# The norms' constant matrix and nineteen other tiles get other places in SBUF

## The chip, the cores and the metric

The kernel runs on one core of a Trainium2 chip. The time is device microseconds of one execution; three executions of the kernel before took 1021.14 to 1021.57 us, with a median of 1021.51 us.

## The reference

Two decoder layers over 256 tokens of width 1024, in float32. Each layer is: half a SwiGLU FFN, a token mixer beside four heads of cross-attention on a memory of 256 tokens, half a SwiGLU FFN. The mixer of the first layer is an mLSTM, that of the second a sliding-window attention.

```python
mem_kv = rms_norm(mem, mem_norm_g) @ mem_w_kv
for i in range(DEPTH):
    x = x + 0.5 * swiglu(rms_norm(x, ffn1_norm_g[i]), ffn1_w_in[i], ffn1_w_out[i])
    hn = rms_norm(x, mix_norm_g[i])
    ...
    x = x + jnp.concatenate([y_tok, y_mem], axis=-1) @ w_out
    x = x + 0.5 * swiglu(rms_norm(x, ffn2_norm_g[i]), ffn2_w_in[i], ffn2_w_out[i])
```

rms_norm(x, g) is x * rsqrt(mean(x*x) + 1e-6) * g, swiglu(x) is (silu(gate) * up) @ w_out with gate and up from x @ w_in (1024 x 5632), and w_out is 2816 x 1024.

## The kernel before

**Matrix products.** Activations lie with features on partitions, 256 tokens in the free dimension. Each float32 factor is split into two float32r parts: weights come from DRAM into a tile wr, ScalarE casts it to wh, VectorE subtracts to get wl; the normed activations are xh and xl, and other activations are split into tiles of the pool up, all named u. A product is three matmuls: wl by xh, wh by xh, wh by xl, each of 128 rows, 128 loaded columns and 256 streamed columns. In `nc.tensor.matmul(out, a, b)` a is loaded into the array (LDWEIGHTS in the profile) and b streams. The profile names a matmul out<-b,a: the streamed operand first, the loaded one after the comma. Most groups load the weights (out<-xh,wl) and stream the activations. Groups with rows=True, in the memory projection and the mixers, load the activations and stream the weights (out<-wl,xh).

**Norms.** The scale of a norm is a sum over features, so over partitions. Norm.square and Norm.fold add up the squares of a token's features per partition (tile acc, a pool of one buffer) and split the result into a tile of the pool up; Norm.chain then multiplies by a 128x128 matrix whose every element is 1/1024, the tile onesr: `nc.tensor.matmul(z, onesr, self.sums[:, i], ...)` for two halves i. There are seven norms, so 14 matmuls that load onesr. The groups that use the norm's result have already begun when these two matmuls run, since the scale is applied to the product; so on TensorE the two stand in the middle of a stream of weight products.

**Small float32 work.** Transposes stream the identity, which is the first 128 columns of the tile con; the cross-attention streams its keys kT and loads its values vM; the sliding-window heads load identb and stream maskb to put a mask into PSUM. These, with onesr, are the tiles of the pool cst that TensorE reads.

**The order.** The program is first noted operation by operation (class Rehearsal). plan() simulates the engines and puts out an order; perform() emits the operations in this order. A tile is a Slot until then: its real tile is asked of its pool when the first operation that names it is emitted (Slot.real). In a pool with several buffers a tag's tiles follow each other through them. In a pool with one buffer, each tag has one place, and the pool gives out places in the order in which it is asked. These pools are cst (20 tags: constants and other tiles that are there once), ap1 (acc) and gp (acol).

**SBUF.** cst begins at byte 16512 of each partition and ends at 29120. Below, a phase is a place modulo 512 bytes, which is the length of one loaded block of 128 float32 columns; the blocks of a tile lie at multiples of 512 from its start, so all of them have one phase. wh and wl lie at phase 0; xh, xl and every u lie at phase 448; these pools do not move.

Of the kernel before, what the change touches and what calls it, by code (L numbers as in the profile page):

```python
# [191 lines left out]
class Rehearsal:  # L192
# [33 lines left out]
    def perform(self, order):  # L226
        nc = self.tc.nc

        def real(x):
            return x.real() if isinstance(x, View) else x  # L230

        for n in order:
            op = self.ops[n]
            getattr(getattr(nc, op.engine), op.kind)(*map(real, op.args), **{k: real(x) for k, x in op.kw.items()})  # L234
# [1261 lines left out]
```

## Time and profile before

| what | before |
|---|---|
| median of three executions | 1021.51 us |
| profiled execution, its own time | 1021.53 us |
| its span, first to last instruction | 1019.7 us |
| mean granted TensorE clock | 0.999 |
| PE busy | 1013.6 us (99%), 8560 matmuls |
| PEld (weight loads) busy | 997.1 us (98%) |
| DVE busy | 664.6 us (65%) |
| ACT busy | 532.0 us (52%) |
| POOL busy | 26.9 us (3%) |

The span is divided like this, by the matmuls in it: memory projection to 32 us, first FFN to about 225, the mLSTM mixer to about 357, second FFN to about 546, third to about 720, the sliding-window mixer to about 838, fourth FFN to the end. The view of stretches gives, for a stretch from A to B us, its length, each engine's busy time in it, in brackets the number of its instructions that touch it, then the granted clock, the share of the DMA engines and GB/s. The duration that the profile gives to a matmul (some 280 ns) is modelled from start to end through a pipeline, and the next one starts long before; what a stream of them costs is the distance from start to start.

### The profile page before, as it was taken

To read this page: it belongs to the slowest core of one execution; us is meant where nothing else is said; L and a number is where in the kernel's file an instruction comes from. 1 tells how busy PE (TensorE), PEld (TensorE's weight loads), DVE (VectorE), ACT (ScalarE), POOL (GpSimd) and SP (SyncE) were. 2 spreads that over 40 slices of the span, in tenths; PEclk is the share of its full clock that TensorE was granted. 3 is DMA by queue.
4 is the path that set the end of the run, shared out by engine and by line. 5 is a ranking of instruction groups with operands and counts; after the bars stand their busy time and mean duration, and the time that the engine had idled before them with its cause. 6 is when DMAs were issued, how large, how long until landed. Compare 5 with 4: busy or idle time off the path is not lost.

```text
span 1019.7 us, 20571 instructions
## 1 busy us (share of the span) xinstructions
PE 1013.6 (99%) x8560; PEld 997.1 (98%) x8560; DVE 664.6 (65%) x1080; ACT 532.0 (52%) x779; POOL 26.9 (3%) x27
## 2 busy tenths in 40 slices
PE   9999999999999999999999999999999999999998
PEld 7999999999999999999999999999998899999998
DVE  6976656678756776655657756556677777656551
ACT  7754544546646644444445444445478765444430
POOL 0020000000000000000000000000113000000000
PEclk9999999999999999999999999999999999999999
DMA  9966665766454476655666666566533437665540
GB/s 322 291 191 200 193 194 173 198 191 180 140 170 145 144 230 186 186 178 175 188 202 189 187 186 187 166 194 192 172 104 125 142 113 223 186 187 176 185 156 22
DMA packets 173204, 182.70 MB, mean 179 GB/s; under 512 B 7124, under 2 KB 168328, under 8 KB 173112
## 3 DMA queue, kind: packets, MB, share of 16 engines
q1 hardware_dynamic: 171872, 179.60, 57.5%
q8 instruction: 67, 1.10, 0.4%
q10 hardware_dynamic: 1016, 1.58, 0.4%
q0 software_dynamic: 224, 0.22, 0.1%
q14 instruction: 25, 0.20, 0.1%
HBM read 180.32 MB, written 1.05 MB: 178 GB/s over the span
## 4 chain that ended last, share of the span: by engine, by line
PE 98%; DMA 1%; SPq 0%; DVE 0%; ACT 0%; issue 0%
PE bank L234 98%; DMA wr<-in_mem_w_kv_dram 1%; SPq L234 0%; DVE wl L234 0%; ACT wh L234 0%; DVE t L234 0%
## 5 line engine op out<-in xcount | busy, mean ns | idle before, releaser
L234 DVE TENSOR_TENSOR wl<-wr,wh 128x1024 fp32r<-128x1024 f32 (+1 forms) x349 | 414.7, 1191 | 282.7 <-ACT wh L234 281.2
L234 ACT CAST wh<-wr 128x1024 fp32r<-128x1024 f32 (+1 forms) x349 | 356.7, 1024 | 413.8 <-PE bank L234 394.7
L234 PE MATMUL bank<-xh,wh 128*128 128x256 f32 x1544 | 432.5, 280 | 0.0
L234 PE MATMUL bank<-xh,wl 128*128 128x256 f32 x1544 | 432.2, 280 | 0.0
L234 PE MATMUL bank<-xl,wh 128*128 128x256 f32 x1544 | 432.0, 280 | 0.0
L234 PE MATMUL bank<-u,wh 128*128 128x256 f32 x1792 | 314.3, 280 | 0.0
L234 PEld LDWEIGHTS bank<-xh,wl 128*128 128x128 f32 x1544 | 293.0, 190 | 0.0
L234 PEld LDWEIGHTS bank<-xl,wh 128*128 128x128 f32 x1544 | 291.6, 189 | 0.1
L234 PEld LDWEIGHTS bank<-xh,wh 128*128 128x128 f32 x1544 | 289.9, 188 | 0.1
L234 PEld LDWEIGHTS bank<-u,wh 128*128 128x128 f32 x1792 | 272.7, 188 | 1.4 <-issue 1.4
L234 PE MATMUL bank<-u,wl 128*128 128x256 f32 x896 | 250.7, 280 | 0.0
L234 PEld LDWEIGHTS bank<-u,wl 128*128 128x128 f32 x896 | 169.8, 190 | 0.5 <-issue 0.5
L234 PE MATMUL bank<-wh,xh 128*128 128x256 f32 x208 | 58.8, 283 | 0.0
L234 PE MATMUL bank<-wh,xl 128*128 128x256 f32 x208 | 58.8, 283 | 0.0
L234 PE MATMUL bank<-wl,xh 128*128 128x256 f32 x208 | 58.5, 281 | 0.0
L234 DVE TENSOR_TENSOR t<-bank,rb 128x256 f32<-128x256 f32 x88 | 36.6, 420 | 14.2 <-PE bank L234 13.9
L234 DVE TENSOR_TENSOR u<-t,u 128x512 fp32r<-128x512 f32 (+1 forms) x59 | 40.4, 685 | 0.3
L234 PEld LDWEIGHTS bank<-wh,xh 128*128 128x128 f32 x208 | 39.1, 188 | 0.1
L234 PEld LDWEIGHTS bank<-wl,xh 128*128 128x128 f32 x208 | 39.0, 188 | 0.1
L234 PEld LDWEIGHTS bank<-wh,xl 128*128 128x128 f32 x208 | 39.0, 188 | 0.1
L234 DVE TENSOR_TENSOR t<-t,bank 128x256 f32<-128x256 f32 x88 | 32.9, 414 | 1.1 <-ACT t L234 1.1
L234 POOL TENSOR_TENSOR col<-col,mhalf 128x4 f32<-128x4 f32 (+2 forms) x15 | 21.8, 1452 | 296.2 <-DVE col L234 296.2
(134 smaller groups left out, 582.0 us busy)
## 6 DMA issues: line engine op xcount, KB each, us to landing
wr<-in_ffn_w_in_dram SPq DMA_DIRECT2D x176, 512.0 KB, 4.5
wr<-in_ffn_w_out_dram SPq DMA_DIRECT2D x80, 512.0 KB, 3.7
wr<-in_a_w_in_dram SPq DMA_DIRECT2D x28, 512.0 KB, 3.7
wr<-in_b_w_in_dram SPq DMA_DIRECT2D x14, 512.0 KB, 4.5
wr<-in_a_w_out_dram SPq DMA_DIRECT2D x12, 512.0 KB, 3.3
wr<-in_b_w_out_dram SPq DMA_DIRECT2D x12, 512.0 KB, 3.4
wr<-in_ffn_w_out_dram SPq DMA_DIRECT2D x16, 256.0 KB, 2.7
wr<-in_mem_w_kv_dram SPq DMA_DIRECT2D x7, 512.0 KB, 7.2
```

What stands on the lines that cost most here:

```text
L234: getattr(getattr(nc, op.engine), op.kind)(*map(real, op.args), **{k: real(x) for k, x in op.kw.items()})
```

## The change

Before the first operation is emitted, every slot that is the first of its tag in a pool with one buffer asks for its real tile, in the order in which the tags were first named in the text. Before, they asked in the order of the plan.

```diff
@@ perform
+        for slots in self.slots.values():
+            if slots[0].pool.bufs == 1:
+                slots[0].real()
         for n in order:
             op = self.ops[n]
```

The instructions, their order on each engine and the semaphores that they wait for are the same in both built programs; only addresses differ. acc and acol stay where they are. The 20 tiles of cst move within the same 12608 bytes. Those that TensorE reads:

| tile | bytes of a partition | read as | place before | phase | place after | phase |
|---|---|---|---|---|---|---|
| onesr | 512 | loaded | 18368 | 448 | 16512 | 128 |
| con (identity at its start) | 1568 | streamed | 16800 | 416 | 17312 | 416 |
| kT0, kT1 | 2048 each | streamed | 23104, 25152 | 64 | 20416, 22464 | 448 |
| vM | 4096 | loaded | 19008 | 64 | 24512 | 448 |
| identb | 256 | loaded | 27264 | 128 | 19136 | 192 |
| maskb | 768 | streamed | 27776 | 128 | 19392 | 448 |

The other tiles of cst (gcol, mhalf, ones, warm, gqk, gcut, gbias, posi, gblk, sink, nsink, rope_s, rope_c) are read by DVE, ACT and POOL alone.

## The prediction

> **What bounds the kernel now.** I read the page's busy shares first, then the chain of work that ended last, then the times that matmuls start (the timeline and the stretches), because only the places of tiles change and TensorE is the engine that reads them most.
>
> ```profile
> PE 1013.6 (99%) x8560; PEld 997.1 (98%) x8560; DVE 664.6 (65%) x1080; ACT 532.0 (52%) x779; POOL 26.9 (3%) x27
> ...
> 11.98 1003.87 PE bank L234 x8516
> ...
> PE bank L234 <- DVE t L234: 1.2, 1, 1.2
> PE bank L234 <- DVE wl L234: 0.8, 1, 0.8
> PE bank L234 <- ACT wh L234: 0.3, 1, 0.3
> ```
>
> The second row is from the chain: one unbroken run of matmuls from 11.98 us on is 1003.87 us of the 1019.7 us span. The last three rows are all that TensorE ever waited for: 2.3 us. So the time is the number of matmuls times the distance between their starts, and a nanosecond in that distance, over the 7944 matmuls of the page's groups of 128x256 (3 x 1544 + 1792 + 896 + 3 x 208), is 8 us. The question is whether that distance is the same everywhere. It is not:
>
> ```profile
> core 0: us, PE busy (x), PEclk, DMA share, GB/s
> 31.87:41.85 9.98, 9.98 (x91) 1.00 1.01 341
> 42.08:69.50 27.42, 27.42 (x235) 1.00 0.68 207
> 75.20:225.37 150.17, 150.17 (x1328) 1.00 0.64 187
> 225.60:238.80 13.20, 13.20 (x115) 1.00 0.77 231
> 239.00:247.60 8.60, 8.60 (x75) 1.00 0.70 188
> 326.00:356.75 30.75, 30.75 (x273) 1.00 0.50 153
> 357.00:545.90 188.90, 188.90 (x1606) 1.00 0.63 193
> 546.20:720.80 174.60, 174.60 (x1484) 1.00 0.61 185
> 721.00:732.20 11.20, 11.20 (x97) 1.00 0.73 222
> 824.00:838.40 14.40, 14.40 (x129) 1.00 0.34 105
> 838.70:1015.40 176.70, 176.70 (x1502) 1.00 0.54 167
> ```
>
> A matmul's modelled 0.28 us reaches over two later starts, so about two in each count began before the stretch. Length over count less two gives the distance: 112.1, 117.7, **113.3**, 116.8, 117.8, 113.5, **117.8**, 117.8, 117.9, 113.4 and 117.8 ns (113.3 and 117.8 from the longest stretches are the ones to trust). There are two paces and nothing between, the granted clock is 1.00 in both, PE is busy throughout in both, and the DMA share is no higher in the slow ones. The same work runs at either pace: 75 to 225 is mostly the first FFN, 357 to 720 the second and third, 838 to 1015 the last. The slow pace shows in the weight loads as well; in every row the name after the comma is the operand that is loaded, the one before it streams:
>
> ```profile
> L234 PEld LDWEIGHTS bank<-xh,wl 128*128 128x128 f32 x357 | 68.5, 192 | 0.0
> ...
> L234 PEld LDWEIGHTS bank<-xh,wl 128*128 128x128 f32 x262 | 49.2, 188 | 0.0
> ```
>
> The first is from 357 to 545 us, the second from 76 to 225 us.
>
> **Where the pace changes.** The stretches begin and end at certain instructions. Here is the first norm's pair of matmuls with the constant matrix, then a return to the fast pace:
>
> ```profile
> 41.62 0.28 PE L234 MATMUL bank<-xh,wh 128*128 128x256 f32 x1
> 41.73 0.28 PE L234 MATMUL bank<-xl,wh 128*128 128x256 f32 x1
> 41.85 0.40 PE L234 MATMUL bank<-u,onesr 128*128 128x256 f32 x2
> 42.08 0.28 PE L234 MATMUL bank<-xh,wl 128*128 128x256 f32 x1
> 42.20 0.28 PE L234 MATMUL bank<-xh,wh 128*128 128x256 f32 x1
> ...
> 252.69 0.28 PE L234 MATMUL bank<-wl,xh 128*128 128x256 f32 x1
> 252.81 0.29 PE L234 MATMUL bank<-xh,wl 128*128 128x256 f32 x1
> 252.94 0.28 PE L234 MATMUL bank<-xh,wh 128*128 128x256 f32 x1
> 253.05 0.28 PE L234 MATMUL bank<-xl,wh 128*128 128x256 f32 x1
> 253.17 0.28 PE L234 MATMUL bank<-xh,wl 128*128 128x256 f32 x1
> ...
> 69.53 0.60 PE L234 MATMUL bank<-con,u 128*128 128x128 f32 x4
> 69.89 0.37 PE L234 MATMUL bank<-xh,wl 128*128 128x256 f32 x1
> 70.09 0.28 PE L234 MATMUL bank<-xh,wh 128*128 128x256 f32 x1
> 70.21 0.28 PE L234 MATMUL bank<-xl,wh 128*128 128x256 f32 x1
> ```
>
> Until 41.85 the starts are 0.11 us apart; the two onesr matmuls and all after them are 0.12 apart. The pace then stays slow until something interrupts the stream: the four transposes at 69.53, or at 252.81 the step from groups that load xh/xl to groups that load wh/wl. The stretches say the same of the other norms: fast before and slow after at 225.4, 356.8 and 838.4, so four norms of four that met the fast pace ended it, and at 545.9 a slow pace stayed slow. So the pace is a state that the stream keeps; loading onesr puts it into the slow one.
>
> Now the places, from the table ahead of this. Operands loaded at phase 0 (wh, wl) run at either pace, as the state has it. Operands loaded at phase 448 (xh, xl at 239.0 and 721.0) run at 117.8 always, and onesr lies at 448 too. What streams cannot be the cause alone: with xh loaded it lies at phase 0, with onesr loaded at 448. **My reading:** a load whose start is not a multiple of 128 bytes (448 is 3.5 times 128) takes some 4.5 ns more than its matmul hides, and leaves the loads behind it late by so much until the stream is broken. A load at a multiple of 128 does neither.
>
> **The change part by part.** No instruction is added, removed or moved, and no tile outside the cst pool gets another place.
>
> *onesr, phase 448 to 128.* By the reading, its 14 matmuls no longer end the fast pace. Between each norm and the next interruption lie, from the counts less two, 233 + 113 + 1604 + 1482 + 1500 = 4932 matmuls at the slow pace. Longest stretches: 188.90 us / 1604 = 117.77 ns and 150.17 us / 1326 = 113.25 ns, 4.52 ns less. 4932 x 4.52 = 22.3 us; the 14 matmuls themselves add 14 x 4.5 = 0.06. The norm at 732.2 stands among loads of xh and gains nothing. No row shows a load at phase 128, so the cost is bounded on both sides: by rows of phase 0 it is −22.3 us, by rows of phase 448 it is nothing. It is nearest to phase 0 by remainder to 128, which is the only common trait of the places that never force the slow pace; I take −22.3 and keep both ends.
>
> *Can the others follow?* In the fast stretch of the first FFN they do:
>
> ```profile
> 75.20:225.37 150.17, 150.17 (x1328) 150.17 (x1326) 95.80 (x130) 73.54 (x90) 0.00 (x0) 1.00 0.64 187
> ```
>
> PE and PEld are busy throughout, DVE 64%, ACT 49%, DMA 0.64. The other three FFNs have the same shapes, so nothing becomes late there; for norms met 4% sooner I add 0.3 us.
>
> *The other 19 tiles.* TensorE reads four:
>
> ```profile
> L234 PE MATMUL bank<-con,u x128: 197/273/329, 69.5 to 817.2; 128*128 128x128 f32 x124, 4*128 4x4 f32 x4
> ...
> L234 PE MATMUL bank<-kT,u x32: 379/379/382, 250.1 to 748.8; 128*128 128x256 f32 x32
> ...
> L234 PE MATMUL bank<-t,vM x32: 378/379/483, 261.1 to 767.1; 128*128 128x256 f32 x32
> ...
> L234 PE MATMUL bank<-maskb,identb x16: 326/331/336, 753.1 to 805.3; 128*128 128x384 bf16 x16
> ```
>
> con keeps phase 416. kT and vM go from 64 to 448, both odd multiples of 64; identb and maskb from 128 to 192 and 448. At 4.5 ns for each of 32 + 32 + 16 that is at most 0.4 us either way; I take 0. What DVE, ACT and POOL read there lies off the chain.
>
> Sum: the profiled execution took 1021.53 us, which is 1.8 us more than its span and 0.02 more than the median, 1021.51. 1021.53 − 22.3 − 0.1 + 0.3 = **999.5 us**.
>
> **Rivals.**
>
> *No change: 1021.5 us.* 128 forces the slow pace as 448 does, because the unit is 256 or 512 bytes, or because what counts is the distance between loaded and streamed operand. For it: wh and wl lie at 0, so the rows cannot tell 128 from 256 or 512, and the distance, 128 − 448, is new too. Against it: it needs a wider unit than the two phases seen call for. Each norm would again be followed by 117.8.
>
> The Trainium skill, "SBUF — State Buffer", section "Who interferes with whom", gives PE one read port for the streamed operand and an independent one for LDWEIGHTS, and says that PE never waits on anyone; by that rule a place within SBUF costs nothing and the time would be 1021.5 us. The trace does not bear it out as it stands: the paces of 113.3 and 117.8 part at a change of the loaded operand alone.
>
> *A re-entry is lost: 1005 to 1015 us.* With norms neutral, the state after an interruption lasts much longer. The stream is broken last at 74.8, 325.7 and 822.4 us; each came back fast. If one comes back slow, it costs from there on: 1326 x 4.52 = 6.0 us less the 0.5 at 225 not won, so 1006; 271 matmuls lost and 3086 not won, 15.2 us, so 1014.7; 127 lost and 1500 not won, 7.4 us, so 1007. For it: some breaks in the mixers ended slow, as in this stretch of loads at phase 0, where 78 matmuls begin and at 113.3 ns 82 would:
>
> ```profile
> 274.60:283.85 9.25, 9.25 (x80) 1.00 0.45 159
> ```
>
> Against it: those three are the same instructions at the same phases as now.
>
> *Slower: 1030 us.* The state after an interruption depends on a place that the change moves: con is 512 bytes higher, kT and vM at another phase. If those breaks then always end slow, and onesr is no better at 128, the fast stretches go: 9.98 + 150.17 + 30.75 + 14.40 = 205.3 us at 117.8 for 113.3, 8.2 us. It decides only if onesr still forces the slow pace or every break fails. Against it: con's phase is unchanged, and the breaks at 74.8, 325.7 and 822.4 have neither kT nor vM near them.
>
> **Chances.** Forecast 0.74; a re-entry lost 0.08; no change 0.13; slower 0.05. 0.2% is about what a measurement of this kernel tells from no change. So faster 0.82, same 0.13, slower 0.05. The forecast's own range is 997.5 (short slow stretches of the mixers come back fast too: some 200 matmuls, 1 us, and 1 us of error in 4.5 ns) to 1002. To hold 8 in 10 it reaches over the lost re-entries to 1015; the end of no change, 1021.5, stays outside with the slower case, 0.18 together.
>
> **What would show it.** Right: the rows from 42, 225.6, 357 and 546 on with starts 113.3 ns apart across the norms, weight loads of wl at 188 in place of 192, loads of xh/xl still 117.8, the same 8560 matmuls. A slow stretch that begins at an onesr row refutes the 128-byte unit; one that begins at a transpose means a lost re-entry; waits of PE on DVE or ACT above 2.3 us mean that the splits no longer keep up.

## The result

The changed kernel takes 999.00 us (median of four, 998.40 to 999.41) against 1021.54 us before (median of four beside it): a ratio of 0.9779, interval 0.9762 to 0.9796. Its profiled execution has a span of 997.0 us, 22.7 less than before.

The same stretches of its trace, TensorE alone (length, busy time and count of matmuls that touch the stretch, granted clock, DMA share, GB/s):

```profile
core 0: us, PE busy (x), PEclk, DMA share, GB/s
9.00:31.20 22.20, 21.16 (x184) 1.00 1.02 352
31.30:41.80 10.50, 10.50 (x91) 1.00 1.06 362
42.10:68.50 26.40, 26.40 (x236) 1.00 0.69 209
74.20:224.30 150.10, 150.10 (x1327) 1.00 0.64 187
224.60:237.20 12.60, 12.60 (x114) 1.00 0.77 224
237.30:245.70 8.40, 8.40 (x77) 1.00 0.77 213
324.10:354.70 30.60, 30.60 (x272) 1.00 0.50 153
355.00:536.70 181.70, 181.70 (x1606) 1.00 0.65 200
537.10:705.00 167.90, 167.90 (x1484) 1.00 0.63 192
705.20:716.00 10.80, 10.80 (x98) 1.00 0.76 237
716.40:719.80 3.40, 3.40 (x31) 1.00 0.52 159
808.00:822.30 14.30, 14.30 (x129) 1.00 0.33 103
822.70:992.70 170.00, 170.00 (x1502) 1.00 0.56 173
```

Length over count less two, as in the prediction, gives the distance from start to start: the two middle FFNs run at 113.3 ns (181.70 / 1604 and 167.90 / 1482) where they ran at 117.8, the last at 113.3 (170.00 / 1500). The pace no longer changes at the norms at 49.1, 224.3, 354.8, 536.8 and 822.4 us.

Three rows are not as forecast. The row groups, which load xh and xl at phase 448, run at 112.0 and 112.5 ns from 237.3 and 705.2 (8.40 / 75 and 10.80 / 96; short counts are good to about 1%, and the starts themselves are 113.4 and 113.3 ns apart), not at 117.8. From 31.3 to 41.8, weight groups that were fast before are slow: 118.0 ns (10.50 / 89); ahead of them, from 13 us on, the memory projection has its starts 113.3 ns apart where they were 117.8. And behind the norm at 716.1, which stands among row groups, the pace is 117.2 ns (3.40 / 29).

Where the 22.7 us come from: 4932 matmuls of the weight groups behind norms, 4.45 ns each, 21.9 us; the row groups at 237 and 705 us, some 170 x 4.4 ns, 0.8; onesr's own matmuls 0.1; the memory projection 0.4, which is some 160 x 4.5 ns less the 0.3 that its stream begins later (12.31 us, before 11.98); less the 90 matmuls from 31.3, 0.4. No norm stands ahead of the memory projection, and in e1 to e6 and e10 to e12, where its operands have the same phases, its trace is slow there; so this part is not shown to come from the change.

The loads of wl between 355 and 536 us are at 188 ns, as forecast, where they took 192 in the slow pace (loads of wh took 188 at either pace):

```profile
L237 PEld LDWEIGHTS bank<-xh,wl 128*128 128x128 f32 x357 | 67.0, 188 | 0.0
```

What TensorE waits for has not grown:

```profile
PE bank L237 <- DVE t L237: 1.2, 1, 1.2
PE bank L237 <- DVE wl L237: 0.8, 1, 0.8
PE bank L237 <- ACT wh L237: 0.3, 1, 0.3
```

### The profile page after: what moved, and what is told of

The parts are those of the page before. It is cut to its first block, busy times and chain, and to the rows that moved or that the text cites. A ratio compares the mean times of both kernels' runs of the same rounds, so it can differ in the third digit from the quotient of the medians.

```text
span 997.0 us, 20571 instructions
## 1 busy us (share of the span) xinstructions
PE 990.9 (99%) x8560; PEld 974.1 (98%) x8560; DVE 664.6 (67%) x1080; ACT 532.8 (53%) x779; POOL 27.0 (3%) x27
## 4 chain that ended last, share of the span: by engine, by line
PE 98%; DMA 1%; SPq 0%; DVE 0%; ACT 0%; issue 0%
PE bank L237 98%; DMA wr<-in_mem_w_kv_dram 1%; SPq L237 0%; DVE wl L237 0%; ACT wh L237 0%; DVE t L237 0%
## 5 line engine op out<-in xcount | busy, mean ns | idle before, releaser
L237 PE MATMUL bank<-xh,wh 128*128 128x256 f32 x1544 | 427.0, 277 | 0.0
L237 PE MATMUL bank<-xh,wl 128*128 128x256 f32 x1544 | 426.7, 276 | 0.0
L237 PE MATMUL bank<-xl,wh 128*128 128x256 f32 x1544 | 426.5, 276 | 0.0
L237 PE MATMUL bank<-u,wh 128*128 128x256 f32 x1792 | 307.3, 277 | 0.0
L237 PEld LDWEIGHTS bank<-xh,wl 128*128 128x128 f32 x1544 | 290.0, 188 | 0.0
L237 PE MATMUL bank<-u,wl 128*128 128x256 f32 x896 | 248.1, 277 | 0.0
```

## The experiments

The row groups at 113 ns speak against the prediction's reason, that a load at an odd multiple of 64 bytes is itself the slow one. The rival taken up is the **distance** between the operand being loaded and the operand that streams at that time: while one matmul streams, the next one's load runs (in the trace of the change a onesr matmul starts at 354.767 us and the next load at 354.770; the load takes 188 ns). A pair is called harmful here when this distance is a multiple of 128 bytes. Weight groups have 0 − 448, row groups 448 − 0, both 64 modulo 128; onesr before had 448 − 448, a multiple of 128, and so had the step from onesr's first to its second load.

**Is it onesr alone?** The first two kernels set places by a list; a number is a gap in bytes. In e1 the places are those of before, onesr's old place is empty and onesr lies behind rope_c at phase 128; e2 has the places of the change and onesr at 448.

```diff
 class Rehearsal: def perform(self, order):
+        cst = self.slots[("cst", "onesr")][0].pool
+        for i, tag in enumerate(PLACES):
+            if isinstance(tag, int):
+                cst.real.tile([P, tag // 4], F32, tag=f"gap{i}", name=f"gap{i}")
+            else:
+                self.slots[("cst", tag)][0].real()
# e1: PLACES = ['gcol', 'con', 512, 'mhalf', ... 'rope_s', 'rope_c', 192, 'onesr', 320]
# e2: PLACES = [512, 'gcol', 'con', ... 'rope_c', 'rope_s', 'onesr', 512]
```

> The places of before, with onesr alone moved to phase 128 (its old place stays empty). If onesr is the whole cause: as the change, 998.5 to 999.5 us, starts 113.3 ns apart across the norms at about 49, 224, 355 and 822 us. If some of the gain comes from the other 19 tiles: between 1000 and 1021 us, and the part that is missing is theirs.

> The places of the change, with onesr alone at phase 448. If onesr is the whole cause: as before, 1021 to 1022 us, 117.8 ns after each norm. If the other 19 tiles carry some of it: below 1020 us by their part.

e1 ran four times and e2 ten times; every kernel from e3 on ran once. The kernel before, beside all of them, took 1021.43 to 1022.49 us.

e1: 999.49 us, ratio to before 0.9785 (0.9770 to 0.9800). e2: 1021.67 us, ratio 1.0001 (0.9992 to 1.0011). So onesr's place carries all of the gain that can be measured, and the other 19 tiles none.

**Which places?** e3, e5 and e4 put onesr at 192, 64 and 256 by the same list as e1, with other gaps around it.

> The places of before, onesr at phase 192, an odd multiple of 64. Theory of the 128-byte unit (the prediction's): it ends the fast pace as 448 did, 1021 to 1022 us. Theory of the distance between loaded and streamed operand (only a load at the phase of the operand that streams meanwhile ends it; 192 - 448 is 256 modulo 512): the pace stays fast, 998 to 1001 us.

> The places of before, onesr at phase 64. So far 448 and 192 end the fast pace, 128 and 256 do not. Odd multiples of 64 end it, whatever the reason (64 - 448 is a multiple of 128): 1021 to 1022.5 us. Only a distance from the streamed operand that is a multiple of 256 ends it (192 and 448 are both that, 64 is not): 998 to 1001 us.

> The places of before, onesr at phase 256, a multiple of 128. 128-byte unit: the pace stays fast, 998 to 1001 us. Distance (256 - 448 is 320): the same. A unit of 512 bytes: 1021 us, since 256 would be off as 448 is.

e3: 1022.28 us. e5: 1021.91 us. e4: 999.04 us. A stretch of 170 us inside the second FFN, from 360 to 530 us in every kernel, shows the pace by its count; first e3, then e5, then e4:

```profile
360.00:530.00 170.00, 170.00 (x1446) 1.00 0.63 192
```

```profile
360.00:530.00 170.00, 170.00 (x1446) 1.00 0.63 191
```

```profile
360.00:530.00 170.00, 170.00 (x1503) 1.00 0.64 197
```

170.00 / 1444 is 117.7 ns, 170.00 / 1501 is 113.3. Phases 64, 192 and 448 end the fast pace, 128 and 256 do not: among multiples of 64, the unit is 128 bytes. A distance counted modulo 512, as e3's rival had it, or 256, as e5's had, is out. The prediction's reason and a distance modulo 128 both still fit, since everything that streams around a norm among weight groups lies at 448.

**Place of the load, or distance?** e6 leaves onesr at 128 and moves what streams past it. The tiles of the split sums are taken from a pool of their own, when they are made; the plan and the order are the same. The diff leaves out the list of places, which is that of the change, and a gap that brings sm to phase 0.

```diff
 class Slot: def real(self):
-            self.made = self.pool.real.tile(shape, dt, tag=tag, name=name)
+            pool = getattr(self, "apart", self.pool)
+            tag = tag if pool is self.pool else "sums"
+            self.made = pool.real.tile(shape, dt, tag=tag, name=name)
 def fold(self):
             self.sums = unit(F32R)
+            self.sums.tile.apart = sm        # sm = pool("sm", 2), at phase 0
```

> The change, but the tile that streams past onesr (the split sums of squares) lies in a pool of its own at phase 0 in place of 448; onesr stays at 128, the order and all else too. If the place of the loaded operand alone decides (a multiple of 128 is harmless): as the change, 998 to 1000 us. If the distance between loaded and streamed operand decides (harmful when a multiple of 128: onesr's second load meets sums at 128 - 0, the next weights' load meets them at 0 - 0): slow after each norm as before, 1020 to 1023 us.

1021.73 us. The stretches before and after the norm at 356.9 us, and the last FFN:

```profile
326.30:356.90 30.60, 30.60 (x272) 1.00 0.51 153
357.30:546.00 188.70, 188.70 (x1605) 1.00 0.64 193
839.00:1015.60 176.60, 176.60 (x1502) 1.00 0.54 167
```

Fast before the norm (30.60 / 270 = 113.3), slow after it (117.7), with onesr where the change has it. The place of the load alone does not decide. What streams past onesr did not decide alone either, since e1 to e5 left it where it was. It is the two together, and their distance modulo 128 fits all of them. e12 is the counterpart: sums at 0 as in e6, onesr at 448, so that the two harmful pairs no longer follow each other.

> The change, sums of squares streamed from phase 0, onesr at 448. Two pairs at a distance of a multiple of 128 again, but no longer in a row: onesr's first load while xh or xl streams, and the next weights' load while sums stream; onesr's second load is 64 away. If any such pair ends the fast pace: slow after each norm, 1020 to 1023 us. If such a pair turns the pace over each time, as at the step from row groups to weight groups in the change (fast to slow at 31 us, slow to fast at 251 us): two of them cancel, 998 to 1001 us.

1022.0 us, slow behind the norms:

```profile
360.00:530.00 170.00, 170.00 (x1446) 1.00 0.62 191
```

So pairs a multiple of 128 apart end the fast pace here too, one apart from the other; that they turn it over each time is out.

**What if every pair is like that, or none exactly?** In e7 the pools of xh, xl, u and v lie 64 bytes higher, in e8 32; a gap behind v returns wh and wl to phase 0. The loop over PLACES is that of e1.

```diff
+PLACES = ['onesr', 'gcol', ... 'rope_s', 64]            # e8: 32; e9: 128
     vp = pool("vp", 2)
+    gapp = pool("gapp", 1)
+    gapp.real.tile([P, 112], F32, tag="gap", name="gap")   # 448 bytes; e8: 480; e9: 384
     wrp = pool("wrp", 5)
```

> The change with the pools of xh, xl, u (and v) 64 bytes higher, so at phase 0; wh and wl stay at 0, onesr at 128. If the place of the loaded operand alone decides: every load is at a multiple of 128, all 8150 matmuls run at 113.3 ns, also the row groups, 995 to 998 us. If the distance decides: every pair is at a multiple of 128, the slow pace is kept up everywhere, 1021.5 plus some 2000 matmuls x 4.5 ns that were fast before, so 1028 to 1032 us, or a third pace.

> The same pools 32 bytes higher, at phase 480: no pair of loaded and streamed operand is then a multiple of 64 apart, and the loads of xh and xl lie at 96 modulo 128. If only exact multiples of 128 in the distance end the fast pace and breaks re-enter at random: 995 to 1000 us. If a load off a multiple of 128 is what costs: the row groups slow, weights as they come, 998 to 1003 us, with slow weights where a break leaves them slow up to 1022.

e7: 1048.37 us. e8: 1034.64 us, above every range that was expected of it. Two FFN stretches and a row group of e7:

```profile
77.00:235.80 158.80, 158.80 (x1326) 1.00 0.60 177
249.60:257.80 8.20, 8.20 (x70) 1.00 0.69 184
371.30:563.60 192.30, 192.30 (x1605) 1.00 0.62 189
```

and of e8:

```profile
76.50:233.10 156.60, 156.60 (x1326) 1.00 0.61 179
246.70:255.00 8.30, 8.30 (x73) 1.00 0.72 195
366.60:556.30 189.70, 189.70 (x1605) 1.00 0.63 192
```

With all loads at multiples of 128 bytes, which the prediction's reason calls best, every float32r matmul takes 120.0 ns (158.80 / 1324; 192.30 / 1603), slower than either pace before, and there is no fast state at all: 49 us more than the change. 32 bytes off, the weight groups take 118.3 ns and the row groups 116.9. Of the distances tried, only 64 modulo 128 has the 113.3. The prediction's reason falls here for good; the distance theory had 1028 to 1032 us for e7 or a third pace, and it is a third pace.

**Is 64 enough to be fast?** e9 moves the same pools by 128, which keeps every distance between them, onesr and the weights modulo 128.

> The change with the pools of xh, xl, u (and v) 128 bytes higher, at phase 64; wh, wl at 0, onesr at 128. If the distance between loaded and streamed operand counts modulo 128, all distances are what they are in the change: 998 to 1001 us. If it counts modulo 256 or 512 as well, the pace of the weight groups is another than 113.3.

1011.06 us, a miss:

```profile
73.60:229.60 156.00, 156.00 (x1327) 1.00 0.61 180
229.90:242.50 12.60, 12.60 (x113) 1.00 0.74 227
291.00:299.60 8.60, 8.60 (x77) 1.00 0.55 173
360.10:541.80 181.70, 181.70 (x1605) 1.00 0.66 200
812.00:827.90 15.90, 15.90 (x137) 1.00 0.35 102
828.20:1005.00 176.80, 176.80 (x1504) 1.00 0.54 166
```

The two paces are the same two, 113.3 (181.70 / 1603) and 117.7 (156.00 / 1325), so the distance counts modulo 128 for them. But the stream came back slow from the transposes before 73.6 us and from the break before 812 us, where the change comes back fast, and it kept that to the norm at 229.6 us and to the end; row groups of the first mixer, slow in the change, are fast here (8.60 / 75, against 119.0 by the starts in the change). What costs 12 us is mainly the re-entry, not the norms. Distance modulo 128 is not all, though: the steps from weight to row groups at 242.5 and 710.1 us end the fast pace (117.8 ns by the starts), where the same steps in the change, with the same distances modulo 128, kept it.

**What decides a re-entry?** e10 and e11 move con, whose identity streams in the transposes, from 416 to phase 0 and 448, by gaps of 96 and 32 bytes ahead of it and the rest of 512 behind it.

> The change with con, whose identity streams in the transposes, at phase 0 in place of 416; all else at its phase. A transpose then has a distance of 64, the step from a transpose to a load of xh has 64 too, and that to a load of wh has 0. If the last pair before a stream decides how it re-enters: row groups come back fast after transposes (up to 2 us less), weight groups slow, above all the first FFN from 74 us and the stream from 325 us: 1000 + 6 + 14, up to 1020 us. If the length of the break decides: 998 to 1000 us.

> The same with con at phase 448: a transpose has distance 0, the step to a load of wh 64, to a load of xh 0. If the last pair decides: weight groups come back fast always, row groups slow as now, 997.5 to 999.5 us. If the length of the break decides: as the change or anywhere up to 1020 us.

e10: 1006.04 us. e11: 999.29 us. In e10 the first FFN came back slow; the short stretch ahead of it (4.00 / 36, 111 ns; 113.3 by the starts) and the stream at 331 us came back fast:

```profile
69.80:73.80 4.00, 4.00 (x38) 1.00 0.92 289
74.60:230.70 156.10, 156.10 (x1328) 1.00 0.62 180
331.80:362.10 30.30, 30.30 (x270) 1.00 0.51 154
```

156.10 / 1326 is 117.7 ns, 30.30 / 268 is 113.1. Before and after the break at 74 us stand the same instructions in e10, e11 and the change, and the same holds at 331 us, so the break's instructions and length alone do not decide; and the last pair, which is the same kind at 69.8, 74.6 and 331.8, does not either. e11 has 999.29 us by either of its expectations and separates nothing. That the place of con bears on the break at 74 us is likely and not shown: with con at 416 or 448 and the rest at these phases, all ten traces came back fast there (before, the change, e1 to e6, e11, e12), but e10 is one run. How it would do so stays open.

## Why the prediction was right, and where its reason was not

**Paces and state: right.** Two paces, kept by the stream from one interruption to the next, and the norms of before ending the fast one: e1 and e2 show it with nothing else changed. In the kernels with a harmful distance between onesr and what streams (before, e2, e3, e5, e6, e12), a norm among weight groups met the fast pace 23 times and ended it 23 times; with a harmless one (the change, e1, e4, e9, e10, e11) it met it 29 times and left it 29 times. These counts are from the starts in the traces.

**The size: right.** Forecast was 22.1 us less, the medians give 22.5. The main term was 4932 x 4.52 = 22.3 us and measured 21.9, since the difference is 4.45 ns. The 0.3 us for waits did not come up. Three terms were missing and partly cancel: the row groups at 237 and 705 us (0.8 gained), the memory projection (0.4 gained) and the first weight groups (0.4 lost). Part of the main term is luck: the stream came to the norm at 41.8 us in the slow pace, which the prediction had not foreseen, and left it in the fast one. Had it stayed slow, as behind the norm at 230.7 us in e10, the 233 matmuls to the next break would have won nothing, 1.0 us.

**The reason: wrong.** The step that failed is "My reading", that a load at an odd multiple of 64 costs more than its matmul hides. Its evidence was that loads at 448 "run at 117.8 always". In the trace of before, each quoted row group stood behind a stretch that a norm had already made slow: 239.0 behind the norm at 225.4, 721.0 behind the slow stretch that began at the norm of 356.8. They inherited the state. With those norms harmless, the same groups at the same phase run at 113. The choice of 128 as harmless "by remainder to 128" came out right by luck: all that streams around a norm among weight groups lies at 448, so there the load's remainder and its distance say the same. Among row groups, where wh and wl stream at 0, onesr at 128 is harmful: in the change the pace goes from 112.5 to 117.2 ns at 716.1 us, as the rows above show, and the same norm does it in e1, e4, e10 and e11. That is "a slow stretch that begins at an onesr row", which the prediction named as the sign against its own 128-byte unit, taken as a unit of the load's place.

**The rivals.** That 128 is as bad as 448 is out, and of its two grounds one was the right kind: it is the distance that counts, but modulo 128, by which 128 − 448 is harmless. The lost re-entry did not occur in the change, but it is real: e10 lost the one at 74 us, for which the prediction had 1006 (6.0 and 0.5 us added to 999.5, though the text says "less"), and took 1006.04 us. Its two main pieces, the 1326 and the 113 matmuls, cost 5.9 and 0.5 us in its trace; that the total agrees so closely is chance, since some 0.6 us of smaller pieces came on top of a time 0.5 us lower than forecast. e9 lost two of the three that the prediction named. The slower case, a place that makes a break come back slow, fits what e10 did with con moved, without onesr being harmful; one run does not show that con was the cause.

The Trainium skill, "SBUF — State Buffer", section "Who interferes with whom", has it that PE's two read ports are independent and PE never waits; by that rule none of these kernels would differ. The paces of 113.3, 117.7 and 120.0 ns, for places of operands alone, do not agree with it. That the two reads collide inside SBUF is an argument from these numbers; no row shows the collision.

**Open.** Why a distance of 64 has two paces, what picks one after a break, and why one single harmful pair, at a step between row and weight groups, ends the fast pace in one place (31.2 us in the change), leaves it in another (237.3) and ends the slow one in a third (252.8 us before); what made the memory projection fast in the change and in e9 and slow in the other kernels. Nor is it known why a harmless norm that meets the slow pace sometimes ends it (41.8 us in the change, 229.6 in e9) and sometimes not (827.9 us in e9, 230.7 in e10), and why the harmful norm among the row groups of e9, which met the slow pace at 721.5 us, left a faster one (114.0 ns). With places at multiples of 64, the runs cannot tell a distance of a multiple of 128 from two places in the same half of 128 bytes. No kernel tried beats the change measurably: e1, e4 and e11 are equal to it.

## What to carry to other kernels

When TensorE is busy throughout, look at the distance from start to start in several stretches; two values for the same work can mean a state that the stream keeps, and the instruction where it flips shows where to look for the cause. In this kernel the best places were those where what is loaded and what streams start 64 bytes apart modulo 128, single small constants in between included: a 512-byte tile used 14 times cost 22 us. Before a row is taken as the cost of its own operands, see what state the rows ahead left.

## What the hardware showed that was not expected

For float32r matmuls of 128 loaded and 256 streamed columns, the distance from start to start depends on the places of the two operands in SBUF modulo 128: on average 120.0 ns at a distance of 0 between them, 118.3 and 116.9 at 32 and 96 (one kernel each), and at 64 either 113.3 or 117.7, kept over more than 3000 matmuls (the slow one in the trace of before from 357 to 732 us, the fast one in the change from 324 to 716 us). Between the best and the worst layout of the same instructions lie 49 us of 1048.
